# A seven-product up projection: a PSUM bank for each product, results in a tile of their own, silu into PSUM, and the four blocks one place later

## The chip, the cores and the metric

One core of a Trainium2 chip runs the whole program. The metric is device microseconds of one execution. The engines are named as in the profile: PE (TensorE matmuls) and PEld (its weight loads), DVE (VectorE), ACT (ScalarE), POOL (GpSimd) and SP (SyncE, which here only issues DMAs).

## What is computed

An encoder layer on 512 tokens of width 1024: a gated delta rule and a pooling branch, merged, and then a channel mixer. The change touches only the first half of the mixer:

```
h2 = rmsnorm(x, norm2_w[l])
u = dwconv_centered(h2 @ ffn_up[l], ffn_conv_w[l], ffn_conv_b[l])
gate, val = jnp.split(u, 2, axis=-1)
x = x + (jax.nn.silu(gate) * val) @ ffn_down[l]
```

`ffn_up` has 2 x 2816 columns (gate and value), the convolution runs over three neighbouring tokens, and the down projection closes the layer. Everything is float32.

## The kernel before

**Products.** Every float32 product is made of three matmuls (`mm3`, L390 to L392): each operand is split into a high part in the matmul's own format, made by ACT as a cast, and a low part, what is left, made by a subtraction on POOL or DVE. The mixer holds tokens along the free axis: the result of the up projection is 128 channels by 512 tokens.

**Blocks.** The up projection runs in 22 blocks `c`. A block makes 128 gate channels and the 128 value channels that belong to them. An ordinary block is two jobs, `up{c}_0` (gate) and `up{c}_1` (value): eight slices of the 1024 inputs, three matmuls of 512 tokens each, in one PSUM bank of the ring `pp` (three banks). Then ACT multiplies by the middle tap of the convolution and adds the bias into a buffer `c3` (ring `cv3`, four buffers), DVE adds the two outer taps (L1968), ACT takes silu of the gate buffer in place (L2200), and DVE multiplies gate by value into the operand `a` of the down projection (L2198). Some splits and sums on `a` for the down projection follow (L1909, L1913, L1922).

**Seven-product blocks.** Four blocks (`SEVEN`: 4, 6, 8, 10) use a scheme of Strassen's kind: the 2 x 2 block product of weights (input half by gate or value) and tokens (input half by token half) is made from seven products of half size instead of eight, each of four slices, three matmuls of 256 tokens. Their order is 1, 2, 6, 5, 7, 4, 3. The sums of weights (`s`, `wr_up`, L1986) and the low parts (L2086) are made per block on POOL and DVE; the token sums are made once (`token_forms`, tiles `as_t` and `tb`). All seven products share one tile of two banks, `ps_w`: products 1, 6 and 4 go one after the other through the same quarter. So ACT copies product 1 and product 1 + 6 out (`keep`, L2145), and DVE adds in four steps (L2154, L2157, L2163, L2160), three of them over two quarters at once. The sums end in `ps_w`, from which the taps read.

**Order of work.** A planner (class `Planner`) takes all tasks with a cost, a key and what they read and write, plays them through on a clock of its own, and so fixes the order of instructions on each engine. Rings of buffers are part of it: a task that opens a buffer waits until one is free. On the chip the order is fixed, and semaphores do the waiting. Besides the up projection, POOL prepares sums of rows of `ffn_down` for the down projection in idle places (`t_unit`, tiles `tp`, L1949), four operations a unit. The weights of ordinary blocks take POOL two operations a job (L421), and ACT one cast (L413).

**PSUM.** Eight banks: three of ring `pp`, three of ring `ds`, and the two-bank tile of ring `oo`. In this stage `ds` is not used.

Of the kernel before, what the change touches and what calls it, by code (L numbers as in the profile page):

```python
# [33 lines left out]
class Task:  # L34
    __slots__ = ("i", "eng", "cost", "fn", "key", "tab", "kb", "preds", "succs", "left", "ready", "news", "uses", "start", "done", "land", "n")


class Planner:
# [50 lines left out]
    def run(self):  # L89
# [40 lines left out]
        while todo:  # L130
# [98 lines left out]
def hybrid_block(  # L229
# [53 lines left out]
    def V(cost, fn, r=(), w=(), key=0.0):  # L283
        add("dve", cost, fn, r, w, key)
# [1630 lines left out]
    def split_part(p, i, n, src, srcn, key):  # L1915
# [61 lines left out]
    SEVEN = (4, 6, 8, 10)  # L1977
# [6 lines left out]
    def fused(eng, cost_n, out, x, y, op, r, w, key):  # L1984
        e, add_, cost = (dve, V, cd(cost_n) + 0.3) if eng == "V" else (pool, G, cp(cost_n))
        add_(cost, lambda: e.tensor_tensor(out=out(), in0=x(), in1=y(), op=op), r=r, w=w, key=key)  # L1986

    def token_forms():
# [30 lines left out]
        def split(f, q):  # L2019
# [3 lines left out]
            def hi():  # L2023
# [20 lines left out]
    def seven_job(c, b):  # L2044
# [30 lines left out]
        def form(f, src, k):  # L2075
# [3 lines left out]
            def hi():  # L2079
# [4 lines left out]
            en, add_, cost = (dve, V, cd(512) + 0.3) if e == "V" else (pool, G, cp(512))  # L2084
            A(ca(512), hi, r=[src[1], "pool:fp"], w=[n], key=feed + 10 + k)
            add_(cost, lambda: en.tensor_tensor(out=wt_[f][:, 1, :], in0=src[0](), in1=f32(wt_[f][:, 0, :]), op=ALU.subtract),  # L2086
                 r=[src[1]], w=[n], key=feed + 10 + k)
# [13 lines left out]
        where = {1: (1, 0), 2: (0, 0), 6: (1, 0), 5: (0, 1), 7: (1, 1), 4: (1, 0), 3: (0, 1)}  # L2101
        on = lambda a, i: f"{o}#{a}{i}"
# [362 lines left out]
```

## Time and profile before

| | |
|---|---|
| runs | 899.82 us median of 3 (899.6 to 900.34) |
| the profiled execution | 896.3 us, its span 894.6 us |
| stage of the up projection with the seven-product blocks | 566 to 673 us of the span |
| granted TensorE clock over the span | 0.996 |

In a timeline row stand the start, the duration, the engine, the source line, the operation, output<-input, shapes, and in brackets the idle time of the engine before it with what ended it. The end of a matmul is modelled: its row shows a duration of 0.28 or 0.39 us, though the next one starts 0.12 or 0.23 later, so distances of starts are the better measure. In a row of groups stand the line, the operation and its shapes, the count, then busy microseconds and mean nanoseconds of one, then idle time before them and its cause. Buffer numbers are left out in the names.

### The profile page before, as it was taken

What the parts mean: (1) busy time and instruction counts of PE and PEld (TensorE: products, weight loads), DVE (VectorE), ACT (ScalarE), POOL (GpSimd) and SP (SyncE); (2) the same over time, 40 slices, a digit from 0 to 9 for tenths busy, and PEclk for the clock granted to TensorE, in tenths of its full rate; (3) what the DMA queues carried; (4) which work ended last, traced back from release to release, by engine and by line L of the source; (5) the groups of instructions that cost most, each with busy time, mean ns of one, the idle gap of its engine ahead of it and who ended that gap; (6) DMA issues with size and microseconds to landing.
All of it is one profiled execution on the core that took longest, in us unless ns stands there. A gap on an engine that the chain in (4) does not pass through costs nothing. (4 is left out here: it accounts for less than half of the span.)

```text
span 894.6 us, 14267 instructions
## 1 busy us (share of the span) xinstructions
PE 868.7 (97%) x5193; PEld 737.5 (82%) x5193; DVE 655.1 (73%) x1076; ACT 487.9 (55%) x839; POOL 570.6 (64%) x476
## 2 busy tenths in 40 slices
PE   9999999999999999999999999789889999999997
PEld 8888888888888888998888897677778878888886
DVE  5767597258578994655767979877767777669996
ACT  6688644337858444266857646444343333465664
POOL 4446455224547564253698979978889987567763
PEclk9999999999999999999999999999999999999999
DMA  7364546313355462135993033444588766366454
GB/s 205 98 212 119 141 117 157 94 49 107 95 148 139 125 141 76 63 119 178 323 343 97 1 95 119 122 150 162 177 267 266 243 217 206 105 204 199 165 178 151
DMA packets 165514, 138.11 MB, mean 154 GB/s; under 512 B 23662, under 2 KB 133051, under 8 KB 165444
## 3 DMA queue, kind: packets, MB, share of 16 engines
q1 hardware_dynamic: 160706, 135.62, 49.2%
q10 hardware_dynamic: 4738, 1.58, 0.8%
q8 instruction: 41, 0.67, 0.3%
q14 instruction: 29, 0.24, 0.1%
HBM read 113.03 MB, written 24.15 MB: 153 GB/s over the span
## 5 line engine op out<-in xcount | busy, mean ns | idle before, releaser
L421 POOL TENSOR_TENSOR wl_up<-wr_up,wh_up 128x512 fp32r<-128x512 f32 x70 | 99.4, 1439 | 29.7 <-ACT wh_up L413 22.6
L392 PE MATMUL ps_up<-h_hi,wl_up 128*128 128x512 f32 (+1 forms) x296 | 112.3, 379 | 1.6 <-POOL wl_up L421 1.5
L390 PE MATMUL ps_up<-h_hi,wh_up 128*128 128x512 f32 (+1 forms) x296 | 112.1, 379 | 0.0
L391 PE MATMUL ps_up<-h_lo,wh_up 128*128 128x512 f32 (+1 forms) x296 | 111.9, 378 | 0.0
L2367 POOL TENSOR_TENSOR w_dn<-wr_dn,w_dn 128x512 fp32r<-128x512 f32 x44 | 66.2, 1519 | 28.4 <-ACT w_dn L2364 25.6
L1968 DVE SCALAR_TENSOR_TENSOR c<-ps_up,fw,c 128x511 f32<-128x511 f32 x72 | 53.8, 747 | 31.2 <-ACT c L1962 29.9
L392 PEld LDWEIGHTS ps_up<-h_hi,wl_up 128*128 128x128 f32 x296 | 55.7, 188 | 13.6 <-POOL wl_up L421 3.1
L391 PEld LDWEIGHTS ps_up<-h_lo,wh_up 128*128 128x128 f32 x296 | 55.7, 188 | 10.1
L390 PEld LDWEIGHTS ps_up<-h_hi,wh_up 128*128 128x128 f32 x296 | 55.7, 188 | 9.9
L1949 POOL TENSOR_TENSOR tp<-tp 128x512 f32<-128x512 f32 x38 | 55.0, 1449 | 1.9 <-DMA t_scr<-tp 0.6
L2364 ACT CAST w_dn<-wr_dn 128x512 fp32r<-128x512 f32 x69 | 42.3, 621 | 24.5 <-PE dn L392 19.9
L391 PE MATMUL dn<-w_dn,as 128*128 128x512 f32 x141 | 54.2, 385 | 0.0
L390 PE MATMUL dn<-w_dn,as 128*128 128x512 f32 x141 | 54.2, 384 | 0.0
L392 PE MATMUL dn<-w_dn,as 128*128 128x512 f32 x141 | 54.2, 384 | 0.0
L1913 DVE TENSOR_TENSOR as<-a,as 128x512 fp32r<-128x512 f32 (+1 forms) x41 | 44.9, 1120 | 3.8 <-ACT as L1909 3.8
L413 ACT CAST wh_up<-wr_up 128x1024 fp32r<-128x1024 f32 x35 | 36.6, 1044 | 11.1 <-POOL tp L1949 5.4
L421 POOL TENSOR_TENSOR wl_k<-wr_k,wh_k 128x512 fp32r<-128x512 f32 x16 | 20.3, 1289 | 28.6 <-ACT wh_k L413 25.7
L421 POOL TENSOR_TENSOR wl_gp<-wr_gp,wh_gp 128x512 fp32r<-128x512 f32 x16 | 22.3, 1416 | 22.2 <-ACT wh_gp L413 22.2
L421 POOL TENSOR_TENSOR wl_v<-wr_v,wh_v 128x512 fp32r<-128x512 f32 x16 | 21.3, 1349 | 22.6 <-ACT wh_v L413 22.6
L421 POOL TENSOR_TENSOR wl_z<-wr_z,wh_z 128x512 fp32r<-128x512 f32 x16 | 20.4, 1294 | 19.8 <-ACT wh_z L413 19.8
L2200 ACT ACTIVATE c<-c 128x512 f32<-128x512 f32 x22 | 13.9, 631 | 34.2 <-DVE c L1968 34.2
L421 POOL TENSOR_TENSOR wl_gd<-wr_gd,wh_gd 128x512 fp32r<-128x512 f32 x16 | 20.7, 1314 | 18.3 <-ACT wh_gd L413 18.3
(526 smaller groups left out, 2877.3 us busy)
## 6 DMA issues: line engine op xcount, KB each, us to landing
wr_up<-in_ffn_up_dram SPq DMA_DIRECT2D x44, 512.0 KB, 4.8
tp<-in_ffn_down_dram SPq DMA_DIRECT2D x22, 512.0 KB, 5.4
t_scr<-tp SPq DMA_DIRECT2D x44, 256.0 KB, 3.4
wr_dn<-t_scr SPq DMA_DIRECT2D x20, 512.0 KB, 3.7
wr_dn<-in_ffn_down_dram SPq DMA_DIRECT2D x15, 512.0 KB, 3.6
x<-in_x_dram SPq DMA_DIRECT2D x8, 512.0 KB, 5.4
wr_k<-in_w_in_dram SPq DMA_DIRECT2D x8, 512.0 KB, 4.8
wr_z<-in_w_in_dram SPq DMA_DIRECT2D x8, 512.0 KB, 3.9
```

Source lines behind the costliest of these rows:

```text
L390: pe.matmul(ps, ahi, bhi, start=first, stop=False)
L391: pe.matmul(ps, ahi, blo, start=False, stop=False)
L392: pe.matmul(ps, alo, bhi, start=False, stop=last)
L413: act.copy(b["hi"], b["raw"])
L421: pool.tensor_tensor(out=b["lo"][:, sl], in0=b["raw"][:, sl], in1=f32(b["hi"][:, sl]), op=ALU.subtract)
L1913: dve.tensor_tensor(out=w[:, :, 1, :], in0=src(), in1=f32(w[:, :, 0, :]), op=ALU.subtract)
L1949: G(cp(512), lambda o=o, x=x, y=y: pool.tensor_tensor(out=w(*o), in0=w(*x), in1=w(*y), op=ALU.subtract), r=[n(*x), n(*y)], w=[n(*o)], key=u)
L1968: dve.scalar_tensor_tensor(out=y[:, lo:hi], in0=box["ps"][:, lo + sh : hi + sh], scalar=fw[:, k, ci : ci + 1], in1=y[:, lo:hi], op0=ALU.mu ...
L2200: A(ca(512), lambda b=b: act.activation(b[0], b[0], AF.Silu), w=[g_], key=u, tab="silu")
L2364: act.copy(b["w"][:, 0, :], raw["t"][:, j, :])
L2367: eng.tensor_tensor(out=b["w"][:, 1, :], in0=raw["t"][:, j, :], in1=f32(b["w"][:, 0, :]), op=ALU.subtract)
```

## The change

A bank for each product: `spot(f)` opens a bank of ring `ds` for every product, and the results go to a two-bank tile `ps_u` of ring `oo`, which only DVE writes. ACT copies product 1 once; six adds of 256 columns follow, each of a product's bank and an SBUF piece, either back to SBUF (`inner`) or to `ps_u` (`outer`). Silu, of all blocks, writes a bank of ring `ds` instead of its own buffer, so that the multiply reads one operand from PSUM. The four blocks are 5, 7, 9 and 11. And the planner reckons a DVE task whose operands are all in SBUF (`ss`) as ending later where POOL is busy, in place of a fixed surcharge.

```
                     cost = t.cost
+                    if t.ss:
+                        cost += max(0.0, free_at.get("pool", 0.0) - now)
...
-        V(cd(256 * n) + 0.15, lambda: part_lo(p, i, n, src), r=srcn, w=names, key=key)
+        V(cd(256 * n) + (0.0 if p in (1, 7) else 0.15), lambda: part_lo(p, i, n, src), r=srcn, w=names, key=key, ss=p in (1, 7))
...
-    SEVEN = (4, 6, 8, 10)
+    SEVEN = (5, 7, 9, 11)
...
-        e, add_, cost = (dve, V, cd(cost_n) + 0.3) if eng == "V" else (pool, G, cp(cost_n))
+        e, add_, cost, kw = (dve, V, cd(cost_n), {"ss": True}) if eng == "V" else (pool, G, cp(cost_n), {})
...
-        where = {1: (1, 0), 2: (0, 0), 6: (1, 0), 5: (0, 1), 7: (1, 1), 4: (1, 0), 3: (0, 1)}
...
-        def spot(a, i):
+        def spot(f):
+            if f not in ps:
+                ps[f] = bank("ds", f"ps_w{c}{f}")
+            return ps[f][:, 0:256]
+
+        def result(j, i):
             if "t" not in ps:
-                ps["t"] = banks2(f"ps_w{c}")
-            return ps["t"][:, a, 256 * i : 256 * i + 256]
+                ps["t"] = banks2(f"ps_u{c}")
+            return ps["t"][:, j, 256 * i : 256 * i + 256]
...
-                M(0.361, lambda k=k: mm(f, k), r=[wn[f], *rname(f, k)], w=[on(*where[f]), f"turn{c}"], key=u + 10 * turn["n"] + k)
+                M(0.361, lambda k=k: mm(f, k), r=[wn[f], *rname(f, k)], w=[pt(f)], key=u + 10 * turn["n"] + k)
...
-        def add_first():
-            dve.tensor_tensor(out=both(0), in0=both(0), in1=twice(pieces(0)[:, 0:1, :]), op=ALU.add)
...
+        def inner(f, dst, x):
+            V(cd(256), lambda: dve.tensor_tensor(out=piece(*dst), in0=spot(f), in1=piece(*x), op=ALU.add),
+              r=[pt(f), pn(*x)], w=[pn(*dst)], key=top)
+
+        def outer(f, dst, x):
+            V(cd(256), lambda: dve.tensor_tensor(out=result(*dst), in0=spot(f), in1=piece(*x), op=ALU.add),
+              r=[pt(f), pn(*x)], w=[on(*dst)], key=top)
+
+        p1, u2, u3, u4 = (0, 0), (0, 1), (1, 0), (1, 1)
         product(1)
-        keep(0)
+        first_kept()
         product(2)
+        outer(2, (0, 0), p1)
         product(6)
-        V(cd(512), add_first, r=[pn[0]], w=[on(0, 0), on(1, 0)], key=top)
-        keep(1)
+        inner(6, u2, p1)
         product(5)
+        inner(5, u4, u2)
         product(7)
-        V(cd(512), add_mid, r=[on(0, 1), on(1, 1), pn[1], "pool:fp"], w=[pn[2], pn[3]], key=top)
+        inner(7, u3, u2)
+        outer(7, (1, 1), u4)
         product(4)
+        outer(4, (1, 0), u3)
         product(3)
-        V(cd(512), add_last, r=[pn[2]], w=[on(0, 1), on(1, 1)], key=top)
-        V(cd(256), add_end, r=[pn[3]], w=[on(1, 0)], key=top)
+        outer(3, (0, 1), u4)
...
-            dve.tensor_tensor(out=a_half(r)[:, i, :], in0=b[0], in1=b[1], op=ALU.mult)
+            dve.tensor_tensor(out=a_half(r)[:, i, :], in0=b["sl"], in1=b[1], op=ALU.mult)
+
+        def silu(c=c, b=b):
+            b["sl"] = bank("ds", f"sl_{c}")
+            act.activation(b["sl"], b[0], AF.Silu)
```

The order moves with it. DVE in a steady block, before (block 8): `w_up8f2`, `f5`, `f4` are low parts of weights, `ps_up7_0` and `ps_up7_1` the jobs of the plain block, L1913 a split for the down projection, L2198 the multiply of gate and value.

```order
L2086 TENSOR_TENSOR w_up8f4_6236<-wr_up8_1_6104,w_up8f4_6236 128x512
L1968 SCALAR_TENSOR_TENSOR c3_29_6251<-ps_up7_1_6174,fw_128,c3_29_6251 128x511 x2
L2154 TENSOR_TENSOR ps_w8_6222<-ps_w8_6222,c3_8_6245 128x2x256
L2198 TENSOR_TENSOR a_0_5498<-c3_7_6200,c3_29_6251 128x512
L1913 TENSOR_TENSOR as_1_5672<-a_0_5498,as_1_5672 128x256
L2157 TENSOR_TENSOR c3_30_6322<-ps_w8_6222,c3_8_6245 128x512
L2163 TENSOR_TENSOR ps_w8_6222<-ps_w8_6222,c3_30_6322 128x256
L2160 TENSOR_TENSOR ps_w8_6222<-ps_w8_6222,c3_30_6322 128x2x256
```

The same place now (block 9); `ps_w92` is the bank of product 2, `sl_8` the silu of block 8, L2155 an inner and L2159 an outer add.

```order
L2088 TENSOR_TENSOR w_up9f4_6344<-wr_up9_1_6221,w_up9f4_6344 128x512
L2159 TENSOR_TENSOR ps_u9_6378<-ps_w92_6351,c3_9_6361 128x256
L1970 SCALAR_TENSOR_TENSOR c3_30_6366<-ps_up8_1_6288,fw_128,c3_30_6366 128x511 x2
L2155 TENSOR_TENSOR c3_9_6361<-ps_w96_6371,c3_9_6361 128x256
L1915 TENSOR_TENSOR as_1_5752<-a_0_5498,as_1_5752 128x256
L2155 TENSOR_TENSOR c3_31_6421<-ps_w95_6395,c3_9_6361 128x256
L2198 TENSOR_TENSOR a_0_5498<-sl_8_6405,c3_30_6366 128x512
L2155 TENSOR_TENSOR c3_31_6421<-ps_w97_6416,c3_9_6361 128x256
L2159 TENSOR_TENSOR ps_u9_6378<-ps_w97_6416,c3_31_6421 128x256
```

Each product now has an add of its own, and the multiply stands between the adds of products 5 and 7. In block 5, the first, the multiply stands later, behind both adds of product 7:

```order
L2155 TENSOR_TENSOR c3_27_5961<-ps_w55_5935,c3_5_5903 128x256
L1915 TENSOR_TENSOR as_1_5752<-a_0_5498,as_1_5752 128x256
L2155 TENSOR_TENSOR c3_27_5961<-ps_w57_5952,c3_5_5903 128x256
L2159 TENSOR_TENSOR ps_u5_5924<-ps_w57_5952,c3_27_5961 128x256
L2198 TENSOR_TENSOR a_0_5498<-sl_4_5932,c3_26_5889 128x512
L2159 TENSOR_TENSOR ps_u5_5924<-ps_w54_5971,c3_27_5961 128x256
```

The banks of `ds` are opened in the order sl_3, products 1, 2, 6 of block 5, sl_4, products 5, 7, 4, 3, then sl_5 and so on, so product 4 follows sl_4 in the same bank. From block 9 on the silu of the plain block opens its bank one product later, so that product 3 follows it.

POOL ahead of the first of the four blocks, before (block 4): `a_0` are token sums, `wl_up3_0` the low parts of an ordinary job's weights.

```order
L1986 TENSOR_TENSOR a_0_5498<-a_0_5498 128x1024 x2
L421 TENSOR_TENSOR wl_up3_0_5651<-wr_up3_0_5569,wh_up3_0_5650 128x512 x2
L1949 TENSOR_TENSOR tp_0_5609<-tp_0_5609 128x512
L421 TENSOR_TENSOR wl_up3_1_5694<-wr_up3_1_5595,wh_up3_1_5693 128x512 x2
L1949 TENSOR_TENSOR tp_0_5609<-tp_0_5609 128x512
```

And now, ahead of block 5:

```order
L1988 TENSOR_TENSOR a_0_5498<-a_0_5498 128x1024
L423 TENSOR_TENSOR wl_up3_0_5652<-wr_up3_0_5569,wh_up3_0_5651 128x512 x2
L1988 TENSOR_TENSOR a_0_5498<-a_0_5498 128x1024
L423 TENSOR_TENSOR wl_up3_1_5694<-wr_up3_1_5595,wh_up3_1_5693 128x512 x2
L1951 TENSOR_TENSOR tp_0_5614<-tp_0_5614 128x512 x2
```

One of the two token sums moved behind the weight of job `up3_0`. The number of matmuls is the same, and the three matmuls of the next plain job that stood ahead of product 3 in each block now stand behind it.

More of the change, by code (lines that the diff above doesn't have):

```diff
@@ L34 @@
 class Task:
-    __slots__ = ("i", "eng", "cost", "fn", "key", "tab", "kb", "preds", "succs", "left", "ready", "news", "uses", "start", "done", "land", "n")
+    __slots__ = ("i", "eng", "cost", "fn", "key", "tab", "kb", "preds", "succs", "left", "ready", "news", "uses", "start", "done", "land", "n", "ss")
 class Planner:
@@ L52, in __init__, with add @@
         self.order = {r: [] for r in rings}
-    def add(self, eng, cost, fn, r=(), w=(), key=0.0, tab=None, kb=0.0, after=(), land=LAND, n=6):
+    def add(self, eng, cost, fn, r=(), w=(), key=0.0, tab=None, kb=0.0, after=(), land=LAND, n=6, ss=False):
         t = Task()
-        t.land, t.n = land, n * 1.012
+        t.land, t.n, t.ss = land, n * 1.012, ss
         t.i, t.eng, t.cost, t.fn, t.key, t.tab, t.kb = len(self.tasks), eng, cost, fn, key, tab, kb
@@ L281, in A, with V @@
         add("act", cost, with_table(tab, fn) if tab else fn, r, w, key, tab)
-    def V(cost, fn, r=(), w=(), key=0.0):
-        add("dve", cost, fn, r, w, key)
+    def V(cost, fn, r=(), w=(), key=0.0, ss=False):
+        add("dve", cost, fn, r, w, key, ss=ss)
     def G(cost, fn, r=(), w=(), key=0.0, after=()):
@@ L1984, in fused @@
     def fused(eng, cost_n, out, x, y, op, r, w, key):
-        e, add_, cost = (dve, V, cd(cost_n) + 0.3) if eng == "V" else (pool, G, cp(cost_n))
-        add_(cost, lambda: e.tensor_tensor(out=out(), in0=x(), in1=y(), op=op), r=r, w=w, key=key)
+        e, add_, cost, kw = (dve, V, cd(cost_n), {"ss": True}) if eng == "V" else (pool, G, cp(cost_n), {})
+        add_(cost, lambda: e.tensor_tensor(out=out(), in0=x(), in1=y(), op=op), r=r, w=w, key=key, **kw)
     def token_forms():
@@ L2124, in mm @@
             sl = slice(k * P, (k + 1) * P)
-            mm3(spot(*where[f]), w[:, 0, sl], w[:, 1, sl], *right(f, k), k == 0, k == 3)
+            mm3(spot(f), w[:, 0, sl], w[:, 1, sl], *right(f, k), k == 0, k == 3)
         turn = {"n": 0}
@@ L2141, in seven_job @@
-        pn = (f"{cg}#0", f"{cg}#1", f"{cv}#0", f"{cv}#1")
+            return b[j][:, 256 * i : 256 * i + 256]
+        pn = lambda j, i: f"{(cg, cv)[j]}#{i}"
         top = FEED - 1e5 + u
-        def keep(i):
-            A(ca(256), lambda: act.copy(pieces(0)[:, i, :], spot(1, 0)), r=[on(1, 0), "pool:fp"], w=[pn[i]], key=top)
-        def both(i):
-            return ps["t"][:, :, 256 * i : 256 * i + 256]
-        def twice(ap):
-            return ap.to_broadcast([P, 2, 256])
-        def add_first():
-            dve.tensor_tensor(out=both(0), in0=both(0), in1=twice(pieces(0)[:, 0:1, :]), op=ALU.add)
@@ L2156, in add_mid, with first_kept @@
-        def add_mid():
-            dve.tensor_tensor(out=pieces(1), in0=both(1), in1=twice(pieces(0)[:, 1:2, :]), op=ALU.add)
-        def add_last():
-            dve.tensor_tensor(out=both(1), in0=both(1), in1=twice(pieces(1)[:, 0:1, :]), op=ALU.add)
-        def add_end():
-            dve.tensor_tensor(out=spot(1, 0), in0=spot(1, 0), in1=pieces(1)[:, 1, :], op=ALU.add)
+        def first_kept():
+            A(ca(256), lambda: act.copy(piece(0, 0), spot(1)), r=[pt(1), "pool:fp"], w=[pn(0, 0)], key=top)
```

20 lines of the change are left out of this document (10 added, 10 removed).

## The prediction

> **What bounds the kernel now.** I read the page first, for the share of each engine, then the PE waits over the whole span, then the busy time of the engines in the four stretches that belong to the seven-product blocks, and last the matmuls themselves in order of time.
>
> ```profile
> span 894.6 us, 14267 instructions
> PE 868.7 (97%) x5193; PEld 737.5 (82%) x5193; DVE 655.1 (73%) x1076; ACT 487.9 (55%) x839; POOL 570.6 (64%) x476
> ```
>
> PE is the bound: it is idle for only 25.9 of 894.6 us, so an edit pays only where it removes one of its waits. The PE waits say where these are (microseconds, times, longest):
>
> ```profile
> PE ps_w L390 <- ACT c L2145: 7.1, 8, 3.3
> PE ps_w L390 <- DVE ps_w L2154: 4.7, 4, 1.3
> PE ps_w L390 <- DVE c L2157: 3.2, 4, 0.9
> PE ps_up L392 <- POOL wl_up L421: 1.5, 2, 1.2
> ```
>
> The first three, 15.0 us, belong to the accumulator that the seven products share (`ps_w`), and to the copy and adds the change rewrites. Next, four stretches, each from the first matmul of a seven-product block to the first of the next pair (a pair is one such block and one plain block): length, then busy time of PE, PEld, DVE, ACT, POOL, the granted clock, and DMA.
>
> ```profile
> 566.42:597.14 30.72, 24.13 (x133) 20.84 (x132) 22.23 (x24) 12.89 (x22) 23.76 (x18) 0.94 0.39 125
> 597.14:622.43 25.29, 22.11 (x134) 19.21 (x132) 18.66 (x21) 11.14 (x19) 21.37 (x16) 1.00 0.50 167
> 622.43:647.72 25.29, 22.11 (x134) 19.21 (x133) 18.65 (x21) 11.14 (x19) 21.37 (x16) 1.00 0.52 167
> 647.72:673.01 25.29, 22.11 (x134) 19.22 (x133) 16.93 (x21) 10.53 (x17) 22.23 (x17) 1.00 0.78 261
> 673.00:750.00 77.00, 76.66 (x337) 62.75 (x336) 58.66 (x61) 29.46 (x41) 70.08 (x52) 1.00 0.75 241
> ```
>
> What a pair would take without a wait comes from the pace of its matmuls, start to start:
>
> ```profile
> 597.14 0.28 PE L390 MATMUL ps_w<-h_hi,w_up6f 128*128 128x256 f32 x1
> 597.50 0.28 PE L390 MATMUL ps_w<-h_hi,w_up6f 128*128 128x256 f32 x1
> ...
> 672.32 0.39 PE L390 MATMUL ps_up<-h_hi,wh_up 128*128 128x512 f32 x1
> 673.00 0.39 PE L390 MATMUL ps_up<-h_hi,wh_up 128*128 128x512 f32 x1
> ```
>
> Three steps in 0.36 us are 0.12 us a narrow matmul; three in 0.68 are 0.227 a wide one. A pair holds 7x4x3 = 84 narrow and 2x8x3 = 48 wide ones: 10.08 + 10.88 = 20.96 us. So the last three pairs lose 25.29 - 20.96 = 4.33 us each, 12.99 together, and the first loses 30.72 - 20.96 = 9.76. That is 22.75 us, more than the idle time of PE shows, because a restarting matmul is booked as busy for longer. The first block also loses clock:
>
> ```profile
> 573.66 0.39 PE L390 MATMUL ps_w<-h_hi,w_up4f 128*128 128x256 f32 x1 [3.33 <-ACT c L2145]
> ...
> 574.48 0.42 PE L391 MATMUL ps_w<-h_lo,w_up4f 128*128 128x256 f32 x1
> ...
> 577.26 0.32 PE L392 MATMUL ps_w<-as_t,w_up4f 128*128 128x256 f32 x1
> ```
>
> After an idle 3.33 us the 17 steps to 577.26 take 0.21 us each instead of 0.12, 1.6 us in all, and the granted clock of the stretch is 0.94.
>
> **The change, part by part.** *One bank a product.* A wait of block 8 shows what goes:
>
> ```profile
> 624.10 0.28 PE L392 MATMUL ps_w<-h_hi,w_up8f 128*128 128x256 f32 x1
> 625.02 0.39 PE L390 MATMUL ps_w<-h_hi,w_up8f 128*128 128x256 f32 x1 [0.64 <-ACT c L2145]
> ```
>
> The block starts at 622.43, so 624.10 is its 15th matmul and the one that waits is the fourth of product 2. Product 2 lies in the other bank than product 1, which ACT copies here; still PE waits, since both are one tile. The waits on L2154 and L2157 are of the same sort: an add over two halves of the tile stops the product after it. With a tile for each product these waits have no reason left. Full recovery: -22.75 us.
>
> *The new waits.* Nine tenants a pair (seven products, two silu) turn through the three `ds` banks, so each waits until the third before it has been read. Which read comes when depends on the queue of DVE; its rows (mean ns of one), with ACT's:
>
> ```profile
> L1913 DVE TENSOR_TENSOR as<-a,as 128x256 fp32r<-128x256 f32 x7 | 9.1, 1296 | 3.8 <-ACT as L1909 3.8
> L1968 DVE SCALAR_TENSOR_TENSOR c<-ps_w,fw,c 128x511 f32<-128x511 f32 x12 | 8.7, 748 | 4.9 <-ACT c L1962 4.7
> L2198 DVE TENSOR_TENSOR a<-c,c 128x512 f32<-128x512 f32 x6 | 7.1, 1188 | 0.1
> L2086 DVE TENSOR_TENSOR w_up8f<-s,w_up8f 128x512 fp32r<-128x512 f32 x1 | 1.8, 1776 | 0.0
> L2154 DVE TENSOR_TENSOR ps_w<-ps_w,c 128x512 f32<-128x512 f32 x3 | 2.1, 689 | 0.0
> L2163 DVE TENSOR_TENSOR ps_w<-ps_w,c 128x256 f32<-128x256 f32 x3 | 1.3, 433 | 3.2 <-PE ps_w L392 3.2
> ...
> L2081 ACT CAST w_up8f<-wr_up 128x512 fp32r<-128x512 f32 x5 | 2.8, 618 | 1.4 <-DVE w_up8f L2086 1.3
> L413 ACT CAST wh_up<-wr_up 128x1024 fp32r<-128x1024 f32 x7 | 7.3, 1044 | 4.7 <-POOL tp L1949 4.6
> L2200 ACT ACTIVATE c<-c 128x512 f32<-128x512 f32 x7 | 4.4, 629 | 6.4 <-DVE c L1968 6.4
> L2145 ACT COPY c<-ps_w 128x256 f32<-128x256 f32 x6 | 2.2, 367 | 11.1 <-PE ps_w L392 11.1
> ```
>
> Take block 9 in its new order, time 0 at its first matmul, a product every 1.44 us, its result there 0.2 later. Before 0 ACT can't cast product 4's weight (its slot is that of the plain job just ending); two casts of 0.62 later, about 1.25, DVE makes its low half, 1.78 long: until 3.0. The add of product 2 then runs from 3.08 to 3.5, the two taps of the plain block to 5.0, the add of product 6 to 5.4: product 7 wants that bank at 5.76, 0.3 to spare. One split (1.30) to 6.7, the add of product 5 to 7.2: product 4 wants the bank at 7.20, nothing to spare. The multiply (0.69) to 7.85, for product 3 at 8.64. The silu before it is ready: copy, cast (1.04), split cast and silu (0.63) on ACT end near 6. So a steady block waits little; I take 0.5 us for each of blocks 7, 9 and 11, between 0 and 1.8 (one more low half ahead of the adds).
>
> Block 5 is ordered otherwise: there the multiply of the silu stands behind both adds of product 7, and product 4 wants its bank. DVE enters that block late (before, too, it had no gap there), so I let the low half of product 4 start at 3.0 instead of 1.25: add of product 2 at 5.0 where product 5 wanted the bank at 4.32 (0.7 lost); then product 7's result at 8.2, two adds to 9.1, the multiply to 9.8, where product 4 stood ready at 7.9 (1.9 lost). 2.6 us, between 0.7 and 4. With three blocks at 0.5 and a restart here and there: 4.3 us.
>
> *The wide adds become six narrow ones* of 0.43, 2.6 us, for three of 0.69 and one of 0.43, 2.5: nothing. The multiply now has one operand in PSUM like L2154; I give it 0.69 for 1.19, so DVE falls from 18.65 to about 17.7 of 20.96. If it kept its length, the place with nothing to spare would lose 0.5 a block, inside the range above.
>
> *GpSimd.* It does the same 15 operations a pair, and takes 21.37 us over them, which is more than PE's 20.96. How it stretches, and its lead:
>
> ```profile
> L1986 POOL TENSOR_TENSOR wr_up<-wr_up,s 128x512 f32<-128x512 f32 x2 | 3.5, 1738 | 0.0
> L1986 POOL TENSOR_TENSOR s<-wr_up 128x512 f32<-128x512 f32 x2 | 2.6, 1290 | 0.0
> ...
> 642.99 1.30 POOL L2086 TENSOR_TENSOR w_up10f<-wr_up,w_up10f 128x512 fp32r<-128x512 f32 x1 [2.27 <-ACT w_up10f L2081]
> ...
> 647.72 0.28 PE L390 MATMUL ps_w<-h_hi,w_up10f 128*128 128x256 f32 x1
> ```
>
> The same subtraction takes 1.29 or 1.74, the long one where DVE works on SBUF operands alone. 15 short ones are 19.4, so 2.0 us of a pair are stretch, over eight such DVE instructions; two of the eight (the multiplies) go: -0.5, between 0 and -0.9 (twice 0.45). About 20.9. And POOL delivers the first weights of a block 3.4 us before PE needs them (644.29 against 647.72), so even 21.37, 0.4 too slow for four pairs, stays within that lead: 0. [...]
>
> *One block later.* The order of POOL changes ahead of block 5, and with it the fourth wait of the list:
>
> ```profile
> 554.20 0.39 PE L391 MATMUL ps_up<-h_lo,wh_up 128*128 128x512 f32 x1
> 555.82 0.50 PE L392 MATMUL ps_up<-h_hi,wl_up 128*128 128x512 f32 x1 [1.24 <-POOL wl_up L421]
> ```
>
> 1.62 for 0.227, and 0.1 on the next: 1.5 us. One of the two wide subtractions ahead of this weight now stands behind it, and block 4 as a plain one puts 10.88 us of PE work under the preparation. -1.5, between 0 and -1.5. Behind the blocks POOL is busy for 70.08 of 77.00 us and PE for 76.66; its table of subtractions for the down weights (`tp`) is as far on as before (20 of them after job 12, 21 before). I add 0.5, between 0 and 2.
>
> *Sum.* -22.75 - 1.5 + 2.6 + 1.5 + 0.2 + 0.5 = -19.45 us. The profiled execution took 896.3 (its span 894.6 and 1.7 around), so 876.85; the median of the runs is 899.82, 3.5 above the profiled one, and I keep that distance: 880.4 us. Everything recovered would be 875.6.
>
> **Rivals.** *GpSimd holds the pairs.* For: 21.37 busy, and in a pair it stood idle 3.9 us for hand-overs from ACT and PE; if half of that stays, a pair takes 23.3: gains 3x2.0, 30.72 - 23.3 less the 0.3 that block 5 exceeds it, 7.1, then 1.5 - 0.5: 14.1, so 885.7; with all of it 893. Against: the lead of 3.4 us. *The banks don't come apart.* Three banks for nine tenants are no bank each; if each block loses what I work out for block 5, 4x2.6, the gain is 24.25 - 10.4 - 0.5 = 13.3: 886.5. For: the place with nothing to spare. *The clock.* Waits between the products could lower it in every block as in block 4: four times 1.6 is 6.3: 886.7. Against: behind the 0.64 above the granted clock of the stretch stays 1.00. [...] *Slower: the queue of DVE.* The adds that hand a bank on stand behind low halves and splits of the other work. If each of products 5, 7, 4 and 3 finds its bank one low half late, 1.78, a block loses 7.1, the four 28.5, and 28.5 + 0.5 - 24.25 = 4.8 us slower: 904.6. It decides from 1.5 us on each of these 16 waits on (24.25/16). For: block 5, where I find 0.7 and 1.9. Against: DVE has 3 us to spare in a pair, so a queue that late would empty before the next block.
>
> **How the numbers follow.** Forecast (gain of 17 to 24) 0.68; GpSimd 0.13; banks 0.10; clock 0.05; queue of DVE 0.03; a loss that just cancels the gain 0.01. 0.2% is 1.8 us, and the three runs span 0.7. Faster 0.96, same 0.01, slower 0.03. The range goes from full recovery, 875.6, to the clock rival, 886.7, with 0.8 more for the distance of median and profile: 887.5. Outside lie the last two cases and the far end of the first rival.
>
> **What would show it.** Right: pairs of 21 to 21.5 us from block 7 on; no wait on ACT's copy; in block 5 waits of PE on L2198; no stretch at a granted clock of 0.94. Wrong: pairs at 23 with POOL ahead of PE's waits (GpSimd), PE waits of over 0.5 on the multiply or adds in every block (banks), matmuls at 0.21 behind short waits (clock), waits of over 1.5 on four products of each block (queue of DVE).

## The result and the profile after

The changed kernel takes 874.27 us (median of 5 runs, 873.37 to 875.08), the kernel before 899.6 (5 runs, 898.41 to 900.34): a ratio of 0.9718, 95% interval 0.9704 to 0.9732, or 25.3 us less. The forecast was 880.4 and its range ended at 875.6; the time lies 1.3 us below that end.

The page of the changed kernel, its span and the busy time of the engines:

```profile
span 873.3 us, 14281 instructions
PE 862.4 (99%) x5193; PEld 734.3 (84%) x5193; DVE 639.7 (73%) x1088; ACT 487.2 (56%) x835; POOL 568.8 (65%) x476
```

The profiled execution took 875.08 us, 21.2 less than that of before; PE is idle for 10.9 us instead of 25.9. All PE waits of the changed kernel of 0.2 us and more (the matmuls stand two lines lower than in before):

```profile
PE pt_warm L622 <- DVE ones L337: 1.1, 1, 1.1
PE pt_a L567 <- DVE xs L556: 1.0, 1, 1.0
PE ps_w L394 <- POOL w_up5f L2088: 0.8, 2, 0.5
PE ps_w L392 <- DVE c L2155: 0.5, 1, 0.5
PE dn L393 <- DVE w_dn L2371: 0.4, 1, 0.4
PE ps_w L392 <- DVE ps_u L2159: 0.2, 1, 0.2
PE dn L393 <- POOL wt_lo L2371: 0.2, 1, 0.2
```

The waits on ACT's copy, on the wide adds and on `wl_up` are gone, and none on the multiply (L2198) has come. By stretch, with the columns of the prediction's table: the four pairs, each from its first matmul, then the plain blocks behind:

```profile
575.19:597.50 22.31, 21.49 (x134) 19.18 (x132) 16.79 (x25) 10.87 (x18) 21.62 (x16) 1.00 0.65 199
597.50:619.16 21.66, 21.45 (x134) 19.19 (x132) 15.63 (x23) 10.54 (x17) 21.50 (x17) 1.00 0.62 205
619.16:640.90 21.74, 21.23 (x134) 19.14 (x132) 17.15 (x25) 10.93 (x18) 21.58 (x16) 1.00 0.62 204
640.90:662.19 21.29, 21.24 (x134) 19.14 (x133) 18.09 (x25) 10.62 (x17) 21.05 (x17) 1.00 0.74 244
662.00:737.00 75.00, 75.00 (x333) 62.10 (x332) 58.55 (x65) 30.64 (x42) 66.50 (x51) 1.00 0.76 249
```

The pairs come to 87.00 us, 3.16 above the 4 x 20.96 they take without a wait. The granted clock is 1.00 in all of them. POOL is busy for nearly all of a pair, which alone tells nothing: it fills its gaps with sums for the down projection.

### The profile page after: what moved, and what is told of

It is laid out like the page before. It is cut to its first block, busy times and chain, and to the rows that moved or that the text cites. A ratio compares the mean times of both kernels' runs of the same rounds, so it can differ in the third digit from the quotient of the medians.

```text
span 873.3 us, 14281 instructions
## 1 busy us (share of the span) xinstructions
PE 862.4 (99%) x5193; PEld 734.3 (84%) x5193; DVE 639.7 (73%) x1088; ACT 487.2 (56%) x835; POOL 568.8 (65%) x476
## 5 line engine op out<-in xcount | busy, mean ns | idle before, releaser
L2371 POOL TENSOR_TENSOR w_dn<-wr_dn,w_dn 128x512 fp32r<-128x512 f32 x44 | 66.7, 1531 | 27.8 <-ACT w_dn L2368 25.9
L1951 POOL TENSOR_TENSOR tp<-tp 128x512 f32<-128x512 f32 x38 | 52.3, 1378 | 0.9
L423 POOL TENSOR_TENSOR wl_v<-wr_v,wh_v 128x512 fp32r<-128x512 f32 x16 | 21.2, 1349 | 22.6 <-ACT wh_v L415 22.6
L393 PEld LDWEIGHTS dn<-w_dn,as 128*128 128x128 f32 x141 | 26.5, 188 | 6.2 <-DVE w_dn L2371 0.9
```

The source lines that it names most:

```text
L393: pe.matmul(ps, ahi, blo, start=False, stop=False)
L423: pool.tensor_tensor(out=b["lo"][:, sl], in0=b["raw"][:, sl], in1=f32(b["hi"][:, sl]), op=ALU.subtract)
L1951: G(cp(512), lambda o=o, x=x, y=y: pool.tensor_tensor(out=w(*o), in0=w(*x), in1=w(*y), op=ALU.subtract), r=[n(*x), n(*y)], w=[n(*o)], key=u)
L2371: eng.tensor_tensor(out=b["w"][:, 1, :], in0=raw["t"][:, j, :], in1=f32(b["w"][:, 0, :]), op=ALU.subtract)
```

## The experiments

Each kernel was run beside the kernel before on the same chip; the medians of before there are 898.9 to 899.1 us.

### Why the runs of before lie above its profile

**Before once more.** No edit.

> The kernel before once more, with a new profiled execution. Open is why the runs of before lie 3.3 us above its profiled execution (899.6 against 896.3) while those of the changed kernel lie 0.8 below theirs. Theory A (clock): the 3.33 us wait in the block 4 costs a stretch of lower clock whose length differs between executions, 1.6 us in the profiled one and some 5 in the usual one. Then the new profile has a wait of 3.2 to 3.4 us on ACT's copy again, and if it takes 899 or more, the excess over 896.3 stands in the stretch from 566 to 600 or right behind it, at a granted clock below 0.94. Theory B (the profiled execution was simply a quick one): the excess is spread over the span, or stands at its start or end, and the stretch of block 4 takes 30.7 us as before.

898.15 us, ratio 0.9996 (0.9979 to 1.0012); its profiled execution took 901.37. The four microseconds behind the 3.33 us wait of block 4, in the profiled execution that the prediction used (first row), and in the new one (four rows; the clock is the third number from the end):

```profile
574.00:578.00 4.00, 3.93 (x21) 3.73 (x19) 1.78 (x2) 2.25 (x3) 4.00 (x3) 0.58 0.20 56
```

```profile
570.00:574.00 4.00, 0.68 (x4) 0.47 (x4) 3.96 (x5) 3.06 (x6) 3.13 (x3) 0.80 0.00 0
574.00:578.00 4.00, 4.00 (x20) 4.00 (x20) 1.78 (x2) 2.24 (x3) 4.00 (x3) 0.50 0.19 50
578.00:582.00 4.00, 2.80 (x12) 2.21 (x11) 3.31 (x4) 0.30 (x1) 3.89 (x4) 0.50 0.98 269
582.00:586.00 4.00, 3.87 (x18) 3.88 (x18) 0.52 (x1) 1.34 (x3) 0.00 (x0) 0.50 0.60 206
...
566.42:600.40 33.98, 27.34 (x133) 23.83 (x132) 22.99 (x24) 12.89 (x22) 23.39 (x18) 0.80 0.35 112
```

The wait is the same to 0.01 us, but this time TensorE runs at half clock for 13.7 us instead of 3.4 (572.4 to 586.1), and the first pair takes 34.0 us instead of 30.72: 3.3 of the 5.0 us by which the spans differ. So far theory A holds in the trace. The other 1.7 us stand behind the four blocks, where PE waits longer for POOL's weights, in the first execution and in the new one:

```profile
728.67 0.50 PE L392 MATMUL ps_up<-h_hi,wl_up 128*128 128x512 f32 x1 [0.28 <-POOL wl_up L421]
```

```profile
727.88 0.50 PE L392 MATMUL ps_up<-h_hi,wl_up 128*128 128x512 f32 x1 [2.02 <-POOL wl_up L421]
```

Of the 63 runs of before that came with a clock, 14 at 0.995 or more have a median of 897.4 us, and 47 at 0.993 or less one of 899.3. The profiled execution of the prediction (896.3 at 0.996) belonged to the quick few; going by the two groups, the clock accounts for some 1.9 us of its distance. That is an inference: a mean clock doesn't say where the clock fell (the changed kernel's profile, at 0.997, has 3.4 us of half clock at 7.6 us, far from the blocks), and how many of the runs have the longer wait on `wl_up` isn't recorded.

**A wait put into the changed kernel.** An instruction is repeated, four times here and seven times in the next run; the result stays what it is.

```
-            add_(cost, lambda: en.tensor_tensor(out=wt_[f][:, 1, :], ...),
+            def low(times):
+                for _ in range(times):
+                    en.tensor_tensor(out=wt_[f][:, 1, :], ...)
+            add_(cost, lambda: low(4 if (c, f) == (SEVEN[0], 2) else 1),
```

> The changed kernel with the low half of product 2's weight in the first of the four blocks (one DVE instruction of 1.1 to 1.8 us, ready 2.7 us ahead of its need) done four times in place of once, to the same result: three more, 3.3 to 5.4 us of DVE, so PE waits 0.6 to 2.7 us there. Theory A (a long wait drops the granted clock to 0.5 for 3 to 13 us): a wait of this size leaves the clock alone in most executions: 875 to 878 us, clock 0.997 or more, runs within 1.7 us. Rival (any wait behind it drops the clock): a stretch at 0.5 as well, over 878.

> As the one before, but done seven times: six more, 6.6 to 10.8 us of DVE, so PE waits 4 to 8 us there. Theory A: a wait of over 3 us drops the granted clock to about 0.5 behind it, for 3 to 13 us, as in block 4 of before; the mean clock of the executions falls to 0.990 to 0.996, the time is the wait plus 0 to 6 us, 878 to 888, and the runs scatter over 2 us or more. Rival (the low clock behind block 4 had another cause): the wait alone, 878 to 882.5, clock 0.997 or more and runs within 1.7 us.

875.26 us (874.83 to 876.67) and 878.94 (878.72 to 880.04). The wait, and the rows behind it, of the first and of the second kernel:

```profile
PE ps_w L394 <- DVE w_up5f L2090: 2.2, 1, 2.2
...
582.00:586.00 4.00, 2.94 (x25) 2.73 (x24) 3.85 (x7) 2.07 (x3) 4.00 (x3) 1.00 0.24 70
```

```profile
PE ps_w L394 <- DVE w_up5f L2090: 4.4, 1, 4.4
...
582.00:586.00 4.00, 3.02 (x14) 3.02 (x15) 3.97 (x6) 1.08 (x2) 3.00 (x3) 0.59 0.02 4
```

2.2 us leave the clock alone here (0.997 or 0.998 in all four runs); 4.4 bring it to 0.59 for a stretch, and the runs to 0.993 to 0.996. The scatter of 2 us that I expected of the second did not come (1.3 over four runs). So the wait of 4.4 us had the low clock behind it, as the 3.33 us of before had in both profiles; how long it then stays low in a given run is not to be foreseen (3.4 and 13.7 us behind the same 3.33). In the first kernel the three pairs behind the wait take 20.98 us each, their floor, where those of the changed kernel take 21.66, 21.74 and 21.29; so the 2.2 us cost only some 1.0 in all.

### Which part of the change is worth what

**The move alone.**

```
-    SEVEN = (4, 6, 8, 10)
+    SEVEN = (5, 7, 9, 11)
```

> Before with the four blocks moved to 5, 7, 9 and 11, and nothing else: still one accumulator of two banks for the seven products. By the theory of the prediction the move is worth the wait on POOL's wl_up, 1.5 us, and the pairs go on losing 4.33 us each on the shared accumulator; block 5 has its weights ready one plain block earlier than block 4 had, so of the 9.76 us lost there between none and 5.4 are won: 892.7 to 898.1 us. Rival (the move did most of it): over 10 us are won and the pairs fall below 23 us. Theory A (clock): if no wait of over 3 us is left in block 5, the profiled execution and the median lie within 1.5 us of each other.

897.03 us, ratio 0.9976 (0.9957 to 0.9995). The pairs from block 7 on take 25.3 us as in before (the first matmuls of blocks 7 and 9 stand at 604.4 and 629.7), and the PE waits of the block are all there:

```profile
PE ps_w L390 <- ACT c L2145: 6.3, 8, 2.5
PE ps_w L390 <- DVE ps_w L2154: 4.6, 4, 1.3
PE ps_up L392 <- POOL wl_up L421: 4.2, 4, 2.2
PE ps_w L390 <- DVE c L2157: 3.1, 4, 0.8
```

The move doesn't touch the shared accumulator, and by itself it doesn't even save the wait on `wl_up`. The runs go from 892.8 to 900.0 us, and median and profile (895.28) lie 1.75 apart, so the hope of a close median and profile failed too. In the profile the clock stays at 1.00 behind the wait of 2.5 us; four of the ten runs stand at 0.993 or 0.994, and where their clock fell isn't recorded.

**All but the move**, in the changed kernel.

```
-    SEVEN = (5, 7, 9, 11)
+    SEVEN = (4, 6, 8, 10)
```

> The changed kernel with the four blocks back at 4, 6, 8 and 10. By the theory of the prediction the banks bring the three pairs behind the first from 25.3 to 21 to 22 us (10 to 13 us), and the first block as well except for what its first weights are late: 875.8 (1.5 us for the wait on POOL's wl_up) to 882 us if block 4 still waits 3 to 5 us for weights. Rival (the banks need the move): block 4 keeps most of its 9.76 us and the time is over 884. Theory A (clock): only if a wait of over 3 us stays in block 4 does the granted clock of that stretch fall below 0.97 and the median lie 2 us or more above the profiled execution.

882.21 us, ratio 0.9808 (0.9793 to 0.9823), 0.2 us above what I expected. The long wait stayed, and theory A then wanted the median 2 us or more above the profiled execution; that took 882.26, so this failed. Block 4 is nearly the whole of the loss, a wait of PE and the row behind it:

```profile
PE ps_w L392 <- DVE a L2198: 4.5, 1, 4.5
...
570.00:574.00 4.00, 3.82 (x23) 3.61 (x22) 0.49 (x1) 1.08 (x2) 4.00 (x4) 0.71 0.43 137
```

Its first product wants the bank in which the silu of an earlier block lies until DVE multiplies it: this is the wait on the multiply that I feared for block 5, in another place and larger. The move avoids it, and so is worth 7.9 us in company and 2.1 alone. The wait on `wl_up` at 555 us is not in this kernel, though its blocks stand where they stood in before.

**All but silu in PSUM.**

```
-            dve.tensor_tensor(out=a_half(r)[:, i, :], in0=b["sl"], in1=b[1], op=ALU.mult)
+            dve.tensor_tensor(out=a_half(r)[:, i, :], in0=b[0], in1=b[1], op=ALU.mult)
...
-            b["sl"] = bank("ds", f"sl_{c}")
-            act.activation(b["sl"], b[0], AF.Silu)
+            act.activation(b[0], b[0], AF.Silu)
```

> The changed kernel with silu written back to its own buffer in SBUF, as before, so that the multiply reads two SBUF operands, and only the seven products turn through the three banks. By the theory of the prediction the multiply takes 1.1 to 1.2 us again instead of 0.68, DVE and POOL are busy some 0.5 us a pair longer, and it costs PE between 0 and 2 us: 874 to 876.3. Rival (the two silu tenants are what makes the products wait): without them the waits on L2155 and L2159 go, 1 us quicker, 873.3.

881.13 us, ratio 0.9795 (0.978 to 0.981): both expectations miss it, by 4.8 us and more. PE now waits for POOL alone in this stage:

```profile
PE ps_up L394 <- POOL wl_up L423: 2.0, 2, 1.1
...
PE ps_w L394 <- POOL w_up5f L2088: 1.1, 1, 1.1
...
```

**Silu in PSUM alone**, in before.

```
-            dve.tensor_tensor(out=a_half(r)[:, i, :], in0=b[0], in1=b[1], op=ALU.mult)
+            dve.tensor_tensor(out=a_half(r)[:, i, :], in0=b["sl"], in1=b[1], op=ALU.mult)
...
-        A(ca(512), lambda b=b: act.activation(b[0], b[0], AF.Silu), w=[g_], key=u, tab="silu")
+        A(ca(512), silu, r=[g_], w=[f"ds:sl{c}"], key=u, tab="silu")
```

> Before with silu into a bank of PSUM, and nothing else; the four blocks at 4, 6, 8 and 10 with the shared accumulator. On top of the banks and the move this edit was worth 6.9 us (881.1 against 874.3), as POOL was then the limit: 22.0 to 22.1 us a pair. Theory P (the edit pays only where POOL sets the pace): here the pairs take 25.3 us and POOL is busy for 21.4 of them, so it brings little: 896.5 to 899.5 us, with the multiply at 0.68 us. Rival (the shorter multiply itself was on the path, by DVE's adds): 2 to 7 us here too, 892 to 897.

889.43 us, ratio 0.9894 (0.9866 to 0.9922): 9.5 us, so theory P falls and the rival is short. Two things may do this: the instruction itself, or the order, which the planner makes otherwise because silu's SBUF buffer comes free earlier. The next two kernels keep the order of all five engines row for row and put only silu's result back into SBUF, from which the multiply reads it again (in the changed kernel with six buffers `c3` for four, so that the order can stand).

```
-            b["sl"] = bank("ds", f"sl_{c}")
-            act.activation(b["sl"], b[0], AF.Silu)
+            act.activation(b[0], b[0], AF.Silu)
```

> The changed kernel with silu in place in SBUF and the multiply reading two SBUF operands, but with every engine's instructions in the order of the changed kernel (two more SBUF buffers stand in for the one that silu no longer frees early). Theory L (length: the multiply of 1.2 us for 0.68, and POOL's instructions stretched beside it): most of the 6.9 us come back, 878 to 882. Theory O (order: silu in PSUM frees its SBUF buffer early, which lets the planner put the next block's weights ahead): with the order kept, 874.3 to 876.

> Before with the order of all engines that silu in PSUM gave it (the run of 889.4 us), but silu's result in SBUF. Theory L: the multiply is 1.2 us again, the pairs go from 24.6 back to 25.3 us and the gain mostly goes: 893 to 898. Theory O: the order alone holds the gain, low halves ahead of the multiply in block 4, no wait of 3.3 us there and no low clock: 889 to 892.

881.69 us, ratio 0.9812 (0.978 to 0.9844), and 898.73, ratio 0.9997 (0.9976 to 1.0018). All of the gain goes back in both: theory L, whose range the second run exceeds by 0.7 us. What the order allows is worth nothing by itself. The multiply and the costliest of POOL's groups between 540 and 673 us, in the changed kernel and in the one with its order and silu in SBUF:

```profile
L2198 DVE TENSOR_TENSOR a<-sl,c 128x512 f32<-128x512 f32 x13 | 8.8, 681 | 0.2
...
L423 POOL TENSOR_TENSOR wl_up<-wr_up,wh_up 128x512 fp32r<-128x512 f32 x33 | 47.9, 1473 | 1.0 <-ACT wh_up L415 1.0
```

```profile
L2198 DVE TENSOR_TENSOR a<-c,c 128x512 f32<-128x512 f32 x13 | 18.4, 1424 | 0.2
...
L423 POOL TENSOR_TENSOR wl_up<-wr_up,wh_up 128x512 fp32r<-128x512 f32 x32 | 49.4, 1564 | 0.9 <-ACT wh_up L415 0.9
...
599.90:621.90 22.00, 21.49 (x134) 19.17 (x132) 16.20 (x24) 10.60 (x17) 21.84 (x16) 1.00 0.58 185
```

The multiply falls from 1.42 to 0.68 us, and these POOL instructions by 0.09 on average. With the slow multiply POOL does 16 instructions in a pair of 22.0 us, 21.84 of them busy, and PE waits for it. Of the 7.0 us between the two profiled spans 2.0 lie in the four pairs, 0.9 in the up projection ahead of them and 3.4 in the plain blocks behind, where all of it stands at matmuls that read POOL's low halves (`wl_up`); the rest lies outside the up projection.

In before, 4.8 of the 9.9 us between the two profiled spans lie in the pair of block 4, 2.0 in the other three pairs and 3.1 in the plain blocks behind, most of it a wait on `wl_up` of 2.40 us, where silu in PSUM leaves 0.61. Block 4 is a matter of DVE's queue ahead of it: the multiplies in the run of that order with silu in SBUF, then in the one with silu in PSUM:

```profile
562.32 3.29 DVE L2198 TENSOR_TENSOR a<-c,c 128x512 f32<-128x512 f32 x2
...
568.38 1.77 DVE L1986 TENSOR_TENSOR s<-s,wr_up 128x512 f32<-128x512 f32 x1
...
572.95 0.36 ACT L2145 COPY c<-ps_w 128x256 f32<-128x256 f32 x1
```

```profile
559.76 1.28 DVE L2198 TENSOR_TENSOR a<-sl,c 128x512 f32<-128x512 f32 x2
...
565.40 1.78 DVE L1986 TENSOR_TENSOR s<-s,wr_up 128x512 f32<-128x512 f32 x1
...
570.09 0.36 ACT L2145 COPY c<-ps_w 128x256 f32<-128x256 f32 x1
```

ACT's casts of the block's weights wait for that sum, and the copy of product 1 stands behind them in ACT's queue. So PE waits 1.28 us for the copy instead of 2.85, and the granted clock stays at 1.00, where behind the 2.85 it is at half for 6.8 us (574.4 to 581.2, a matmul every 0.21 us for 0.12).

**All but the banks**: before with silu in PSUM, as above, and the move.

```
-    SEVEN = (4, 6, 8, 10)
+    SEVEN = (5, 7, 9, 11)
```

> Before with the blocks moved to 5, 7, 9 and 11 and silu in PSUM; the seven products keep their shared accumulator and its four waits a block. With silu alone (889.4) the matmuls of a block start 0.62, 0.95, 0.62 and 0.94 us late on it, 3.13 together; four blocks lose 12.5 by it where the changed kernel's four lose 3.2 in all, so 9.3 us above the changed kernel, plus up to 2 for a wait on wl_up: 883 to 886 us. Rival (the banks are worth little once the multiply is short, since the time then goes to POOL instead): 875 to 880.

889.0 us, ratio 0.9882 (0.9848 to 0.9917): 3 us above what I expected. The waits are the expected four a block, but each costs a restart of PE as well (the step after the first matmul behind a wait takes 0.22 us in place of 0.12), so that a pair takes 24.6 us (603.2 to 627.8), 3.64 above 20.96, and the wait on `wl_up` is 1.8. The PE waits:

```profile
PE ps_w L390 <- ACT c L2145: 4.0, 8, 0.8
PE ps_w L390 <- DVE ps_w L2154: 3.2, 4, 0.8
PE ps_w L390 <- DVE c L2157: 3.1, 4, 0.8
...
```

Put last, the banks are worth 889.0 - 874.3 = 14.7 us, silu 881.1 - 874.3 = 6.9, the move 7.9. (The kernel without the banks has the old reckoning of the planner, too, which is worth 0.9 below.) They add to 29.5 where the change brings 24.8 (899.1 - 874.3), so they are not independent; most of what the move brings, for one, is a wait that the banks and silu themselves would bring to block 4.

### Whether the shared tile was the reason, and the number of banks

**Products 1 and 2 in the two halves of one bank**, in the changed kernel.

```
-            if f not in ps:
-                ps[f] = bank("ds", f"ps_w{c}{f}")
-            return ps[f][:, 0:256]
+            t = 1 if f == 2 else f
+            if t not in ps:
+                ps[t] = bank("ds", f"ps_w{c}{t}")
+            return ps[t][:, 256:512] if f == 2 else ps[t][:, 0:256]
```

> The changed kernel, but products 1 and 2 of a block lie in the two halves of one bank tile. The prediction says that PE waited for ACT's copy of product 1 because the next product stood in the same tile, not because it needed the copy. By that, product 2 waits for the copy again in each of the four blocks, some 0.8 us lost each time (624.10 to 625.02 in before, less 0.12), 3.2 together: 877 to 878 us, with waits of PE on ACT's copy at the start of product 2 in the trace. Rival (the waits came from the ring of banks or from late data, and not from the shared tile): no wait on ACT's copy, 873.8 to 875 us.

876.8 us (876.32 to 878.91), ratio 0.9755 (0.9727 to 0.9784). As the theory has it, the wait on the copy is back once in every block, 0.46 us in three and 1.47 in block 7; it costs some 2.5 us where I had expected 3.2:

```profile
PE ps_w L392 <- ACT c L2153: 2.9, 4, 1.5
```

**Two banks in the ring.**

```
-        "pp": 3, "ds": 3, "oo": 1, ...
+        "pp": 3, "ds": 2, "oo": 1, ...
```

> The changed kernel with two banks in the ring in place of three, for the same nine tenants a pair. Each tenant then waits until the second before it has been read. By the prediction's reckoning of block 9 the add of product 2 ends 0.6 us after product 6 began and the adds behind a low half or a split (1.78 and 1.30 us of DVE) come 1 us or more late: 2 to 5 us a block, 882 to 894 us, with PE waiting on L2155, L2159 and L2198. Rival (the three banks are not what brings it, only that the adds write elsewhere): 874 to 877 us.

919.49 us, ratio 1.0243 (1.0198 to 1.0287), far outside the expectation, and mostly not for the reason in question: earlier stages use the ring `ds` too, PE now waits in several of them, and the up projection begins 24.4 us later (542.0 for 517.6).

```profile
PE ps_up L394 <- POOL wl_up L423: 6.3, 5, 2.3
PE pt_a L567 <- DVE h_lo L575: 4.6, 4, 1.4
```

The four pairs take 101.3 us, 14.3 more than in the changed kernel, but with POOL's weights late (6.3 us of waits on `wl_up`) and a granted clock of 0.95 from 535 to 710 us. So the run doesn't tell what the third bank is worth to the products.

### The planner's reckoning, and attempts to do better

**The old reckoning in the changed kernel.**

```
-                    if t.ss:
-                        cost += max(0.0, free_at.get("pool", 0.0) - now)
...
-        e, add_, cost, kw = (dve, V, cd(cost_n), {"ss": True}) if eng == "V" else (pool, G, cp(cost_n), {})
+        e, add_, cost, kw = (dve, V, cd(cost_n) + 0.3, {"ss": True}) if eng == "V" else (pool, G, cp(cost_n), {})
...
```

> The changed kernel with the planner's old reckoning of DVE: fixed surcharges of 0.3 and 0.15 and no allowance for a busy POOL; the order on DVE, ACT and POOL comes out otherwise. The prediction gave the reckoning no term of its own. By that, no more than a wait or two change: 873.3 to 876 us. Rival (the reckoning is what keeps low halves and splits out of the way of the adds that hand a bank on, and of POOL): waits of PE of 0.5 us and more on L2155, L2159 or POOL's weights in most blocks: 877 to 884 us.

875.21 us (874.34 to 877.29). The reckoning only trades waits: a wait of 1.79 us on `wl_up` at 555.93 us is back, and behind it the clock fell in this execution, to 0.65 from 558 to 562 us; but the pairs of blocks 5 and 7 take 21.0 us, their floor:

```profile
PE ps_up L392 <- POOL wl_up L421: 1.8, 1, 1.8
...
558.00:562.00 4.00, 4.00 (x14) 3.18 (x13) 3.96 (x6) 0.81 (x2) 4.00 (x5) 0.65 0.60 192
...
579.00:600.00 21.00, 21.00 (x134) 19.10 (x133) 16.95 (x23) 10.90 (x19) 20.22 (x16) 1.00 0.65 198
```

The wait at 555 us stands in the profile of every kernel with the old reckoning, also where the blocks are moved (1.22 us with the move alone, 1.78 without the banks), and of none with the new one, also where they are not. POOL's queue shows why: here both wide token sums stand ahead of this weight (`up3_0`), while under the new reckoning only one of them does, even with the blocks at 4, 6, 8 and 10 (second row):

```profile
547.92 5.75 POOL L1986 TENSOR_TENSOR a<-a 128x1024 f32<-128x1024 f32 x2
```

```profile
548.28 2.40 POOL L1988 TENSOR_TENSOR a<-a 128x1024 f32<-128x1024 f32 x1
```

**The old surcharges only where they seemed to help**: for the low halves in blocks 7, 9 and 11, and in the second kernel for the splits too (last two lines).

```
+            if e == "V" and c > SEVEN[0]:
+                cost, kw = cd(512) + 0.3, {}
...
-        V(cd(256 * n) + (0.0 if p in (1, 7) else 0.15), lambda: part_lo(p, i, n, src), ..., ss=p in (1, 7))
+        V(cd(256 * n) + 0.15, lambda: part_lo(p, i, n, src), ...)
```

> The changed kernel with the old surcharge of 0.3 for the low halves of DVE in blocks 7, 9 and 11, the new reckoning elsewhere; POOL's order is that of the changed kernel up to its 221st row, so no wait on wl_up at 555 us comes back. If the pairs of 21.0 us in the run with the old reckoning came from these low halves: 872 to 873.8. Rival (they came from the order on POOL and the splits, which stay here): 873.8 to 876.

> As the one before, and the low parts of the splits with their old surcharge of 0.15 too. Theory: pairs of 21.0 to 21.3 us from block 7 on, 871.8 to 873.8. Rival: an order with waits of its own, among them the one on wl_up at 555 us: 874 to 877.

875.31 us (874.28 to 878.22) and 876.66 (874.98 to 877.67): the rivals in both, though the wait on `wl_up` that the second rival names did not come. Each new order has a wait of its own, 0.6 us on the copy in block 7 of the first, 1.2 on an add (L2161) there in the second.

**One more sum on DVE.** The second kernel has `"GVGV"`.

```
-    SUM_ENG = "GVGG"
+    SUM_ENG = "GVVG"
```

> The changed kernel with one more of the four sums of a block (the third, a21) on DVE in place of POOL: POOL has 1.4 to 1.8 us less a pair, DVE 0.7 to 1.8 more (17 of 21.7 us before). Theory P (POOL, busy for 21.5 of 21.7 us of a pair, still sets the pace of the changed kernel): the pairs fall towards 21.0 us: 871.8 to 873.8 us. Rival (POOL's lead covers it and the adds on DVE are what PE waits for): the longer queue of DVE costs 0 to 1 us a block: 874.3 to 878.

> As the one before, with the fourth sum (a12) on DVE in place of POOL. It is needed last, for the weight of product 3. Theory P: 871.8 to 873.8 us. Rival: 874.3 to 878, with PE waiting on L2155, L2159 or on the low half of product 3.

876.89 us (876.55 to 877.26) and 880.02 (879.38 to 880.88). POOL is relieved in the first (busy for 18.93 us of block 7's pair of 22.56, where the changed kernel has 21.50 of 21.66), and the time is longer: theory P is wrong here as well, and the second lies above its rival's range too. PE waits for the copy and an add in the first, for an add and still for POOL's weights in the second:

```profile
PE ps_w L392 <- ACT c L2152: 1.4, 1, 1.4
PE ps_w L392 <- DVE c L2155: 1.3, 1, 1.3
```

```profile
PE ps_up L394 <- POOL wl_up L423: 2.5, 2, 1.8
PE ps_w L392 <- DVE c L2155: 1.9, 2, 1.7
```

None of these beats the changed kernel.

## Why the prediction was wrong in size and right in sign

**The step that failed: "the median of the runs is 899.82, 3.5 above the profiled one, and I keep that distance".** In the changed kernel the median lies 0.8 below its profiled execution. That is 4.3 of the 6.1 us between 880.4 and 874.27. I carried the distance over as if it were a property of every program. What the second profile of before shows in its place are two costs that the first has in small and the changed kernel not at all: half clock for 13.7 us behind block 4's wait instead of 3.4, which is 3.3 us, and a wait on `wl_up` behind the blocks of 2.02 us instead of 0.28, which is 1.7. The prediction named the drop of the clock and priced it at 1.6 us, from one execution; of the other wait its profile had only the 0.28. By the two groups of runs the clock makes 1.9 of the 4.3 us; how the remaining 2.4 divide between the wait on `wl_up` and the scatter of single executions, on either side, stays open. Without the distance the forecast would have been 876.85 and its lower end 872.1, with the time between them.

**The new waits were 1.1 us too large.** Block 5 was to lose 2.6 us to the bank of product 5 and to the multiply; it lost 1.35, all of it at two waits for POOL's weights, and never waited for the multiply. The other three lost 0.70, 0.78 and 0.33, 1.81 together where I took 1.5, and mostly on the adds, as said. With the restarts that is 3.16 for 4.3.

**The stretch behind: +0.5, and near by luck.** The plain blocks behind take 1.0 us less than in before (which has one more of them, taken off at 10.88), since they no longer wait for POOL's weights, and the down projection 1.4 more, with waits on its weights that before hasn't (0.43 and 0.16 us): +0.4 by two parts that the prediction didn't have. The profiled spans differ by 19.6 us in the pairs, 1.4 in the up projection ahead of them (which now has the one more), less this 0.4, and by 0.7 before the up projection begins, where other kernels scatter as much: 21.3 us.

**Full recovery of 22.75 us: right in the main, with one price wrong.** The waits on the shared tile did go because the tiles came apart: the run with products 1 and 2 in one bank brings one of them back, and with the banks and the move, but the multiply in SBUF, the pairs still take 89.0 us instead of 106.6. (The 22.75 also holds two waits of block 4 on low halves, 0.53 and 0.55 us, which have nothing to do with the tile; two of that kind, 0.55 and 0.28, are what block 5 still has.) But the prediction costed the multiply from PSUM at nothing for PE, with "0" for GpSimd behind its lead of 3.4 us. Without that edit, in the same order, the pairs take 22.0 to 22.9 us, PE waits on POOL's weights, and 7.4 us are lost, more of them in the plain blocks behind than in the pairs. So the rival "GpSimd holds the pairs" is, in a mild form, what the banks without silu in PSUM do. The lead did not cover it, since POOL feeds the plain blocks as well (PE's waits on `wl_up` come to 1.6 us in that run). Between 540 and 673 us the multiply takes 0.68 us on average with one operand in PSUM and 1.42 with both in SBUF, and POOL's `wl_up` instructions 1.47 and 1.56.

**One block later: -1.5. The number right, the owner wrong.** The wait on `wl_up` is gone, and the up projection is 1.4 us quicker ahead of the blocks. The prediction read the cause rightly (one of the two wide instructions ahead of the weight now stands behind it), but this order comes from the planner's reckoning, for which it had no term, and not from the move: moved blocks with the old reckoning keep the wait. The move is worth 7.9 us in company for another reason, because block 4's first product would find its bank taken.

**The rivals.** The queue of DVE and the banks stayed within the forecast's own bounds; the two runs with one more sum on DVE show that they are near: 2.6 and 5.7 us slower. The clock rival fell as argued: the longest wait in the four blocks is 0.55 us, the granted clock there is 1.00, and the runs stand at 0.997 to 0.999.

## What to carry to other kernels

Compare the profiled execution with the runs before making the sum against it: if the runs scatter or lie apart, take a second profile, look for the waits that differ and for a long PE wait with low clock behind it (here 3.33 us, with half clock for 3.4 us in one profile and for 13.7 in the other), and count these too as gain where the change removes them. Where a change has several parts, say for each term which part it hangs on, and test that by leaving the part out: the wait on `wl_up` belonged to the part that had no term. For an operand moved from SBUF to PSUM, look at the other engines and at every queue behind it as well: here the multiply on DVE fell from 1.42 to 0.68 us, POOL's `wl_up` instructions in the same stretch from 1.56 to 1.47, and the kernel from 881.69 to 874.27. To find what an edit of a planned kernel is worth, keep the order and change only the instruction.

## What the runs showed of the hardware

- These PE waits had low clock behind them, or from before their end on: 3.33 us in both profiles of before (half clock for 3.4 us in one, 574.0 to 577.4, and for 13.7 in the other, 572.4 to 586.1), 2.85 in before with the order of silu in PSUM (half clock for 6.8 us), 4.4 with the repeated instruction (0.59 from 582 to 586 us), 4.5 with the banks and without the move (0.86 from 566 to 570 us, 0.71 from 570 to 574) and 1.79 on `wl_up` with the old reckoning (0.65 from 558 to 562 us). These had not: the 2.2 put in (1.00 from 578 to 590 us), the 2.50 of the move alone (a matmul every 0.12 us behind it), and 1.78 at the place of the 1.79 in two kernels, silu in PSUM alone and all but the banks (1.00 in both). So the length of the wait alone doesn't settle it.
- A lower mean clock needn't show in the time: the kernel with the banks at blocks 4, 6, 8 and 10 has two runs at 0.993 and two at 0.996, and both groups take 881.9 to 883.0 us. Where the clock fell in the runs without a profile isn't recorded.
- Behind a wait PE loses some 0.1 us more: the step after the first matmul takes 0.22 us in place of 0.12 (582.58 to 582.80 with the move alone), among wide matmuls 0.34 in place of 0.23 (555.93 to 556.27 with the old reckoning).
- In these kernels a matmul's wait goes by the PSUM tile: with two products in the two halves of one bank tile, the second waits for the copy of the first, 0.46 us in three blocks, though it doesn't touch it, and in before it does so (0.64) with the two in different banks of one tile. Whether the hardware or the semaphores placed for the tile ask for this, no run tells.
